# Nineteen column groups of an input projection by Strassen's seven products, ahead of the attention, their results kept in DRAM

## Chip, cores, metric

The kernel runs on one core of a Trainium2 chip. The metric is device time in microseconds (us): the median of the runs of one launch. Engines: PE (TensorE), DVE (VectorE), ACT (ScalarE), POOL (GpSimd), SP (SyncE, which here only issues DMAs).

## The reference

An encoder block on 1024 tokens of 1024 channels, all float32. A modulated RMSNorm gives `h`; one projection feeds two branches, which are merged by sigmoid gates, projected and added to the input.

```python
proj = h @ w_in        # 1024 x 9232
q_a, k_a, v_a, o_a, z_a, gates, q_b, k_b, v_b, z_b, g_merge = split(proj)
q_a, k_a = split(silu(conv3(concat(q_a, k_a))))
h_a = sigmoid(o_a) * bidirectional_mlstm(q_a, k_a, v_a, gates)   # 4 heads of 256
y_a = rms_norm_per_head(h_a) * silu(z_a)
y_b = neighbourhood_attention(q_b, k_b, v_b) * silu(z_b)         # 8 heads of 64
gm = sigmoid(g_merge + b_merge)                                  # two branches
merged = gm[0] * (y_a @ w_proj_a) + gm[1] * (y_b @ w_proj_b)
out = rms_norm(x + gate * (merged @ w_out))
```

The mLSTM is computed by chunks of 256 tokens: within a chunk as masked scores, between chunks through a state C of 256 x 256 a head, forward and backward.

## The kernel before

Every matrix product is made from float32 operands split in a high and a low part (`hi`, `lo`), as three PE products (`mm3`); `h` is held transposed as eight tiles `hhi`, `hlo` [128 channels, 1024 tokens]. `w_in` comes in groups of 256 columns. SP loads two of the eight row tiles at a time (`wraw`), ACT makes `whi`, POOL makes `wlo`. `dense_cm` computes a group channel-major, with moving operands of 512 columns (96 matmuls, four PSUM banks `dps`), `dense_tm` token-major, with moving operands of 256 columns (192 matmuls).

The PE order is written by the program (`manual_schedule`); the other engines' orders are made by a scheduler, and each engine works its instructions off in that order. The PE order comes from `weave`: it emits a **fill**, the dense groups, and between their steps the parts of the **chains** (generators), each when the lag it asked for, counted in us of emitted matrix work, has passed, or when a named flag is set. Where the fill waits for a flag, the chain's parts follow each other with nothing in between.

The stages, by PE's order:

- `front`: the norm, `h` and the gate columns, with the first group (`QB`, `KB` of pair 0).
- `na`: the attention. Chain `na_chain`: 64 blocks of 128 queries, each `na_scores` (tile `sps`, one bank; DVE adds the bias and takes the maximum, ACT the exponential, DVE normalises into `pt`), `na_weights` (three transposes `tps`, ACT and DVE split them into `ptr`) and `na_values` (`ops`). Fill `na_fill`: for each of four pairs a `VB`/`ZB` group, a merge gate group `gmerge(1, pair)`, the next pair's `QB`/`KB` group, at last `gmerge(0, 0)`.
- `projb`: branch B's projection, ahead of it `gmerge(0, 1)`; the chain `gates` makes the mLSTM's decays.
- `branch_a`: the mLSTM. Chain `mlstm`, for each head: backward states (`kps` transposes, `kweighted`, `state_step` into `cps`), then chunks c = 0 to 3 (`ml_scores` into `sps`, `Dm` and its split `pm`; products with the states and with v into `ips`; numerators `num`, divisors `rd`, sum `hout`). Fill `ml_fill`: per head K, V, Q groups, of the head before the O and Z groups (`gated_out`, token-major, whose evacuations apply the gates and the norm), and two `gmerge(0, ..)`.
- `proj_a`, `out_proj`: projection, merge, output projection, final norm.

The lags that set how closely chain parts stand:

```python
LAG = 1.1
NLAG = 0.6
```

Of the kernel before, what the change touches and what calls it, by code (L numbers as in the profile page):

```python
# [12 lines left out]
F32 = mybir.dt.float32  # L13
# [6 lines left out]
P = 128  # L20
# [25 lines left out]
class Build:  # L46
# [4 lines left out]
    # ---------------------------------------------------------------- helpers  # L51
# [96 lines left out]
    def dense_cm(self, src, cols, rhs, evac, nk=NK, nst=NST):  # L148
        """As dense_cm_steps, each bank in turn over a part's nst rows of tiles."""
# [16 lines left out]

    def dense_tm(self, src, cols, lhs, evac):
        """Token-major: 256 columns; bank b holds token tiles 2b and 2b+1."""
# [20 lines left out]
    # ---------------------------------------------------------------- constants  # L189
# [48 lines left out]
    # ---------------------------------------------------------------- adaLN RMSNorm, h^T  # L238
    def front(self, cols):
        """h^T, with the first projection (256 columns) and that of the gates following its tiles."""  # L240
        nc, io = self.nc, self.io
        got = []
        with self.pool("fr", bufs=2) as fp:
            wv = io["w_ada"].rearrange("(p j) (s k n) -> p j s k n", j=8, s=3, k=8)
# [90 lines left out]
            def h_high(s):  # L335
                x, m = xnT[:, 0, s], md[0]
                self.v0 = fp.tile([P, 512], F32, name="v0")
# [14 lines left out]
            xnT = fp.tile([P, NK, T], F32, name="xnT", bufs=1)  # L352
# [111 lines left out]
            self.constants()  # L464
# [20 lines left out]
    def gate_rows(self, ps):  # L485
        """Pre-activations, a row per direction and head; the backward ones in reversed time.
        Those of the lo parts of the weights lie four rows on."""
        nc = self.nc
        self.li = self.ybp.tile([40, T], F32, name="li")
        self.lz = self.ybp.tile([40, T], F32, name="lz")  # L490
# [80 lines left out]
    def out_gate(self, fp):  # L571
        """Half the residual gate as a row in DRAM."""
# [32 lines left out]
    # ---------------------------------------------------------------- neighbourhood attention  # L605
    def na(self, first, gps, ps0, ps1, fill):
        nc, io = self.nc, self.io
        self.yb = [self.ybp.tile([P, T], F32, name=f"yb{p}") for p in range(4)]
        with self.pool("na") as np_:
# [7 lines left out]
            for a in range(2):  # L617
                for h in range(2):
                    self.na_qk(0, a, h, first[a])
            self.gate_rows(gps)  # L620
            ps0.close()
# [5 lines left out]
    def na_fill(self):  # L627
        io = self.io
        for pair in range(4):
# [4 lines left out]
            yield from self.gmerge(1, pair)  # L634
            if pair < 3:
                yield from self.dense_cm(io["w_in"], [(QB + (pair + 1) * P, P), (KB + (pair + 1) * P, P)], self.hT,
                                         lambda a, h, banks: self.na_qk(pair + 1, a, h, banks))
# [46 lines left out]
    def na_chain(self):  # L684
        """Blocks of 8 columns of queries of each head: scores, then weights, then values."""
# [49 lines left out]
    def na_head(self, pair, hh):  # L735
        """Tables of 8 * bias + mask, rows of keys beside those of queries."""
# [94 lines left out]
    def projb(self, pp):  # L831
# [6 lines left out]
        yield from self.gmerge(0, 1)  # L838
# [15 lines left out]
    # ---------------------------------------------------------------- mLSTM  # L854
    def conv(self, mp, banks, ct, out):
        """3-tap convolution over tokens and x * (1 + tanh(x / 2)), which is 2 silu(x)."""
        nc = self.nc
        up = mp.tile([P, T + 2], F32, name="up", tag="up", bufs=2)
        nc.gpsimd.memset(up[:, 0:1], 0.0)
        nc.gpsimd.memset(up[:, T + 1:T + 2], 0.0)  # L860
        for h in range(2):
            nc.scalar.copy(up[:, 1 + h * 512:513 + h * 512], banks[h])
        yc = mp.tile([P, T], F32, name="yc", tag="yc")
# [472 lines left out]
```

## Time and profile before

| | |
|---|---|
| runs | 1330.67, 1331.93, 1332.37 us (median 1331.93) |
| profiled execution, first to last instruction | 1329.1 us |
| PE busy | 1305.2 us, 98%, 7560 matmuls |
| DVE, ACT, POOL busy | 651.8, 566.7, 418.5 us |
| HBM traffic | 92.48 MB read, 20.08 MB written |

The profiled execution gives its span; the median of the runs is 2.8 us above it. The costliest groups are the matmuls into `dps` (the dense groups). A matmul's duration in the profile holds its way through the array, so the pace of a row of matmuls is read from start to start.

### The profile page before, as it was taken

What the parts mean: (1) busy time and instruction counts of PE and PEld (TensorE: products, weight loads), DVE (VectorE), ACT (ScalarE), POOL (GpSimd) and SP (SyncE); (2) the same over time, 40 slices, a digit from 0 to 9 for tenths busy, and PEclk for the clock granted to TensorE, in tenths of its full rate; (3) what the DMA queues carried; (4) which work ended last, traced back from release to release, by engine and by line L of the source; (5) the groups of instructions that cost most, each with busy time, mean ns of one, the idle gap of its engine ahead of it and who ended that gap; (6) DMA issues with size and microseconds to landing.
All of it is one profiled execution on the core that took longest, in us unless ns stands there. A gap on an engine that the chain in (4) does not pass through costs nothing.

```text
span 1329.1 us, 19861 instructions
## 1 busy us (share of the span) xinstructions
PE 1305.2 (98%) x7560; PEld 1127.5 (85%) x7560; DVE 651.8 (49%) x1381; ACT 566.7 (43%) x1191; POOL 418.5 (31%) x381
## 2 busy tenths in 40 slices
PE   8799999999999899999999999999999999999997
PEld 8677777777777688988999989999989989888886
DVE  6944536435345441347626654555625641533533
ACT  6564434334444412336424553364434543423322
POOL 2634434335324423222212222222222212153332
PEclk9999999999999999999999999999999999999999
DMA  9633222222223364112111121112111122446432
GB/s 291 155 88 92 72 61 72 76 56 72 69 66 95 107 208 119 48 41 72 46 42 44 45 73 48 41 44 77 40 40 45 44 80 86 160 136 196 160 101 89
DMA packets 106187, 116.24 MB, mean 87 GB/s; under 512 B 9724, under 2 KB 86012, under 8 KB 106092
## 3 DMA queue, kind: packets, MB, share of 16 engines
q1 hardware_dynamic: 97352, 102.69, 27.1%
q10 hardware_dynamic: 8740, 12.29, 2.7%
q8 instruction: 59, 0.97, 0.3%
q14 instruction: 36, 0.29, 0.1%
HBM read 92.48 MB, written 20.08 MB: 85 GB/s over the span
## 4 chain that ended last, share of the span: by engine, by line
PE 91%; DMA 3%; DVE 2%; SPq 1%; ACT 1%; issue 1%; POOL 0%; ACTq 0%; POOLq 0%; DVEq 0%
PE dps L79 67%; PE ops L79 8%; PE ips L79 5%; PE sps L79 4%; PE cps L79 3%; PE tps L83 1%; PE wps L83 1%; DMA t_d<-gtmp 1%; SPq L251 1%; DMA wor<-in_w_out 1%; DMA wa<-in_w_ada 1%; PE kps L83 0%; PE ytp L83 0%; DVE acc L280 0%; PE gaps L79 0%
## 5 line engine op out<-in xcount | busy, mean ns | idle before, releaser
L74 POOL TENSOR_TENSOR wlo<-wraw,whi 128x512 fp32r<-128x512 f32 x168 | 227.0, 1351 | 585.9 <-ACT whi L73 576.0
L79 PE MATMUL dps<-hhi,whi 128*128 128x512 f32 x768 | 318.7, 415 | 1.0 <-ACT gtmp L827 0.6
L79 PE MATMUL dps<-hhi,wlo 128*128 128x512 f32 x768 | 302.6, 394 | 0.0
L79 PE MATMUL dps<-hlo,whi 128*128 128x512 f32 x768 | 298.8, 392 | 0.0
L79 PE MATMUL dps<-whi,hhi 128*128 128x256 f32 x768 | 217.1, 283 | 0.0
L79 PE MATMUL dps<-wlo,hhi 128*128 128x256 f32 x768 | 217.1, 283 | 0.0
L79 PE MATMUL dps<-whi,hlo 128*128 128x256 f32 x768 | 217.0, 283 | 0.0
L73 ACT ACTIVATE whi<-wraw 128x512 fp32r<-128x512 f32 x168 | 105.6, 629 | 228.6 <-PE dps L79 186.5
L79 PEld LDWEIGHTS dps<-hhi,whi 128*128 128x128 f32 x768 | 145.3, 189 | 32.2 <-issue 10.6
L79 PEld LDWEIGHTS dps<-hhi,wlo 128*128 128x128 f32 x768 | 145.2, 189 | 32.3
L79 PEld LDWEIGHTS dps<-hlo,whi 128*128 128x128 f32 x768 | 145.3, 189 | 18.6 <-DVE hlo L342 0.4
L79 PEld LDWEIGHTS dps<-wlo,hhi 128*128 128x128 f32 x768 | 146.9, 191 | 0.2
L79 PEld LDWEIGHTS dps<-whi,hhi 128*128 128x128 f32 x768 | 146.9, 191 | 0.2
L79 PEld LDWEIGHTS dps<-whi,hlo 128*128 128x128 f32 x768 | 146.9, 191 | 0.0
L79 PE MATMUL dps<-ya,whi 128*128 128x512 f32 x256 | 79.3, 391 | 0.0
L768 ACT ACTIVATE pt<-pt,mx 128x384 f32<-128x384 f32 (+1 forms) x64 | 37.7, 589 | 94.6 <-DVE mx L766 94.2
L1052 POOL TENSOR_TENSOR dg<-negm,mmask 128x256 f32<-128x256 f32 x32 | 25.0, 781 | 98.7 <-issue 28.9
L79 PEld LDWEIGHTS dps<-ya,whi 128*128 128x128 f32 x256 | 47.6, 188 | 9.7 <-DVE t0r L1182 0.2
L79 PE MATMUL ops<-woh,mlo 128*128 128x512 f32 (+1 forms) x136 | 51.3, 377 | 0.0
L79 PE MATMUL ops<-wol,mhi 128*128 128x512 f32 (+1 forms) x136 | 51.2, 377 | 0.0
L79 PE MATMUL ops<-woh,mhi 128*128 128x512 f32 (+1 forms) x136 | 51.2, 377 | 0.0
L79 PE MATMUL dps<-ya,wlo 128*128 128x512 f32 x128 | 49.9, 389 | 0.0
(265 smaller groups left out, 2359.1 us busy)
## 6 DMA issues: line engine op xcount, KB each, us to landing
wraw<-in_w_in SPq DMA_DIRECT2D x112, 256.0 KB
wa<-in_w_ada SPq DMA_DIRECT2D x16, 512.0 KB
wraw<-in_w_in SPq DMA_DIRECT2D x64, 128.0 KB
t_d<-gtmp ACTq DMA_DIRECT2D x32, 256.0 KB
xt<-in_x SPq DMA_DIRECT2D x8, 512.0 KB
wag<-in_w_ada SPq DMA_DIRECT2D x16, 256.0 KB
t1r<-t_d SPq DMA_DIRECT2D x8, 512.0 KB
mp_d<-t1r SPq DMA_DIRECT2D x16, 256.0 KB
```

What stands on the lines that cost most here:

```text
L73: nc.scalar.activation(hi, raw, AF.Copy)
L74: nc.gpsimd.tensor_tensor(lo, raw, f32(hi), op=ALU.subtract)
L79: self.nc.tensor.matmul(out, lhsT=lhsT, rhs=rhs, start=start, stop=stop, skip_group_check=True)
L83: self.nc.tensor.transpose(out, src, ident)
L251: nc.sync.dma_start(wa[:, :, s, :], wv[:, :, s, k, :])
L768: nc.scalar.activation(p_, p_, AF.Exp, bias=mx, scale=-1.0, accum_out=sm)
L1052: nc.gpsimd.tensor_tensor(dg, negm.rearrange("p (a b) -> p a b", a=2), mk, op=ALU.add)
```

## The change

Nineteen groups (three of `gmerge(1, ..)`, and K, O, Q, Z of four heads) are computed right after the front, before the attention, by Strassen's scheme (Winograd's form). `h` is cut in four quarters (channels by tokens), a group of `w_in` likewise; `combos` makes four sums of quarters of `h` once, as hi and lo; `st_set` computes one group by seven products of 12 matmuls, each 512 columns wide. Each group's result goes through its `put` function (tanh, silu or the convolution) to DRAM: `t_d`, `o_d`, `z_d`, `k_d`, `q_d`. `gmerge(1, 0)` is the front's group now, `gmerge(0, 1)` follows the front, and pair 0's `QB`/`KB` group begins the attention's fill. In the mLSTM only V remains a dense group (`values`). K and Q come back by chunk (`chunk`), O and Z too, in a new `gated_out`, spawned as a chain of its own after each chunk: O is transposed on PE (`otp`), multiplied in, squared, normed, and transposed back (`ytp`).

```diff
@@ new, called before the attention
+    def combos(self, x):
+        for k in range(4):
+            a11, a12, a21, a22 = x(k, 0), x(k + 4, 0), x(k, 1), x(k + 4, 1)
+            t = [sp.tile([P, 512], F32, name="part", tag="part", bufs=6) for _ in range(4)]
+            nc.vector.tensor_tensor(t[0], a22, a21, op=ALU.subtract)
+            nc.vector.scalar_tensor_tensor(t[1], t[0], -1.0, a11, op0=ALU.mult, op1=ALU.subtract)
+            nc.vector.tensor_tensor(t[2], a11, a21, op=ALU.subtract)
+            nc.vector.scalar_tensor_tensor(t[3], t[1], -1.0, a12, op0=ALU.mult, op1=ALU.subtract)
+            for i in (1, 0, 2, 3):
+                hi, lo = [s[:, k] for s in self.S[i]]
+                nc.scalar.activation(hi, t[i], AF.Copy)
+                (nc.gpsimd if i % 2 else nc.vector).tensor_tensor(lo, t[i], f32(hi), op=ALU.subtract)
+    def st_set(self, c0, put, psum):
...
+        x = bank()
+        yield from product(x, split(w11), quarter(0, 0), True)
+        p1 = copied(x)
+        y = bank()
+        yield from product(y, split(w21), quarter(1, 0), True)
+        put(0, 0, y, p1, False)
+        t1 = total(w11, w12)
+        t2 = total(t1, w22)
+        yield from product(x, split(t2), summed(1), False)
...
+        put(0, 1, x, None, False)
+    def ahead(self):
...
+            for g in range(1, 4):
+                do(GM + 1024 + g * 256, self.put_tanh(self.t_d[1], g, 8 + g * 2))
+            for hd in range(HEADS):
+                do(KA + hd * 256, self.put_conv(self.k_d[hd], 8 + hd * 2))
+                do(OA + hd * 256, self.put_tanh(self.o_d, hd, None))
+                do(QA + hd * 256, self.put_conv(self.q_d[hd], hd * 2))
+                do(ZA + hd * 256, self.put_silu(hd))
@@ na_fill
+        yield from qk(0)
         for pair in range(4):
...
             if pair:
                 yield f"na{pair - 1}"
-            yield from self.gmerge(1, pair)
             if pair < 3:
...
@@ projb
-        yield from self.gmerge(0, 1)
@@ mlstm
-        nxt = self.ml_split(mp, 0, qT, kT)
+        nxt = self.ml_split(mp, 0, qd, kd)
...
+            self.spawn(self.gated_out(mp, hd, c, hout))
@@ gated_out, now by chunk
+        for src, n in ((self.o_d, "oc"), (self.z_d, "zc")):
+            t = mp.tile([P, 2, L], F32, name=n, bufs=2)
+            nc.sync.dma_start(t, src[hd * 256:(hd + 1) * 256, s].rearrange("(a p) t -> p a t", p=P))
...
+        yield 3.0
...
+                self.transpose(tp[:, i, dt], oz[0][:, dt, i * P:(i + 1) * P], self.ident)
+        for i in range(2):
+            nc.vector.scalar_tensor_tensor(hout[:, i], tp[:, i].rearrange("p a b -> p (a b)"), 1.0, hout[:, i], op0=ALU.add, op1=ALU.mult)
+            so = mp.tile([P, 256], F32, name="so", bufs=2)
+            nc.scalar.activation(so, hout[:, i], AF.Square, accum_out=ssq[:, i:i + 1])
+        self.rsqrt(rstd, ssq, 1.0 / HD, 4 * EPS, mp, 2)
+        for i in range(2):
+            nc.scalar.activation(hout[:, i], hout[:, i], AF.Copy, scale=rstd[:, i:i + 1])
+        last = hd == HEADS - 1
+        yield "ya" if last else 6.0
...
@@ ml_fill
-        gm = [[2], [], [], [3]]
-        for hd in range(HEADS):
-            yield from self.qkv(mp, hd)
-            if hd:
-                yield from self.gated_out(mp, hd - 1)
-            for g in gm[hd]:
-                yield from self.gmerge(0, g)
-        yield "ml3"
-        yield from self.gated_out(mp, 3)
+        yield from self.values(mp, 0)
+        yield from self.values(mp, 1)
+        yield from self.gmerge(0, 2)
+        for hd in range(2, HEADS):
+            yield f"ml{hd - 2}"
+            yield from self.values(mp, hd)
+            if hd == 3:
+                yield from self.gmerge(0, 3)
```

Three places of the built program. In the attention, PE's order of the kernel before, in the middle of pair 0 (`dps` are steps of the fill, the rest is the chain):

```order
L79 MATMUL dps<-hhi_104,whi 128x512
L79 MATMUL dps<-hlo_105,whi 128x512
L79 MATMUL dps<-hhi_104,wlo 128x512
L79 MATMUL sps<-kB,qA 128x384
L79 MATMUL sps<-kl,qA 128x384
L79 MATMUL dps<-hhi_90,whi 128x512
L79 MATMUL dps<-hlo_91,whi 128x512
L79 MATMUL dps<-hhi_90,wlo 128x512
L83 MATMUL tps<-ident,pt 128x128 x3
```

PE's order of the change, near the end of pair 0:

```order
L79 MATMUL ops<-ptr_3952,vb 128x256
L79 MATMUL ops<-ptr_3953,vb 128x256
L79 MATMUL sps<-kB,qA 128x384
L79 MATMUL sps<-kl,qA 128x384
L83 MATMUL tps<-ident,pt 128x128 x3
L79 MATMUL ops<-ptr_3952,vb 128x256
L79 MATMUL ops<-ptr_3953,vb 128x256
L79 MATMUL sps<-kB,qA 128x384
L79 MATMUL sps<-kl,qA 128x384
```

The fill stands no longer between the parts of some blocks: five at the end of each pair, and the last blocks' weights and values behind them.

In the mLSTM, PE's order of the kernel before in chunk 2 of head 0 (products with the backward state, then the state's update):

```order
L79 MATMUL ips<-sb2h,qsh 128x258
L79 MATMUL ips<-sb2l,qsh 128x258
L79 MATMUL ips<-sb2h,qsl 128x258
L79 MATMUL dps<-hhi_94,whi 128x512
L79 MATMUL dps<-hlo_95,whi 128x512
L79 MATMUL dps<-hhi_94,wlo 128x512
L79 MATMUL cps<-vhi,kwh 128x258
L79 MATMUL cps<-vlo,kwh 128x258
```

PE's order of the change at the same place:

```order
L79 MATMUL ips<-sb2h,qsh 128x258
L79 MATMUL ips<-sb2l,qsh 128x258
L79 MATMUL ips<-sb2h,qsl 128x258
L79 MATMUL ips<-sb2h,qsh 128x258
L79 MATMUL ips<-sb2l,qsh 128x258
L79 MATMUL ips<-sb2h,qsl 128x258
L79 MATMUL cps<-vhi,kwh 128x258
L79 MATMUL cps<-vlo,kwh 128x258
```

The steps of the fill between the two are gone; the next `dps` stands after the last chunk of the head.

ACT's order of the change in a chunk without fill (head 1, chunk 2; in brackets whose work each waits for):

```order
L1226 ACTIVATE so,hssq<-hout 128x256 [waits DVE_49] x2
L1229 ACTIVATE hout<-hout,hrstd 128x256 [waits Activation_49,Pool_49]
L1229 ACTIVATE hout<-hout,hrstd 128x256 [waits Activation_49]
L1163 ACTIVATE hout<-num,rd 128x256 [waits DVE_49]
L1137 ACTIVATE num<-ips,col_6842 128x258 [waits PE_49]
L1137 ACTIVATE num<-ips,col_6842 128x258 [waits PE_49,Activation_49]
L1056 ACTIVATE qsh<-qc 128x512
```

The two scalings by `hrstd`, which come from the new `gated_out` of the chunk before and wait for POOL's root, stand ahead of this chunk's `num` and of `qsh`, which the next chunk's scores need.

## Rows read from the trace of the kernel before

**Rows 1.** The page: span, and part 1's row of PE.
```profile
span 1329.1 us, 19861 instructions
...
PE 1305.2 (98%) x7560; PEld 1127.5 (85%) x7560; DVE 651.8 (49%) x1381; ACT 566.7 (43%) x1191; POOL 418.5 (31%) x381
```
**Rows 2.** The chain of waits in order of time: start us, us, what, count.
```profile
148.80 16.34 PE dps L79 x72
...
611.01 1.42 PE sps L79 x12
...
626.58 1.43 PE sps L79 x12
...
1098.74 42.86 PE dps L79 x358
```
**Rows 3.** PE in order of time (start us, us), four transposes and what follows.
```profile
724.27 0.60 PE L83 MATMUL kps<-ident,kT 128*128 128x128 f32 x4
...
724.62 0.36 PE L79 MATMUL dps<-whi,hhi 128*128 128x256 f32 x1
```
**Rows 4.** Busy time by stretches, two chunks of head 0.
```profile
611.00:627.00 16.00, 16.00 (x105) 14.53 (x104) 12.96 (x35) 9.21 (x22) 4.32 (x4) 1.00 0.26 67
627.00:643.00 16.00, 16.00 (x105) 14.54 (x104) 9.84 (x30) 8.21 (x19) 2.71 (x3) 1.00 0.14 33
```
**Rows 5.** DVE and POOL in order of time, chunk 1 of head 0.
```profile
611.96 1.52 DVE L1026 SCALAR_TENSOR_TENSOR hout<-num,rd,hout 128x256 f32<-128x256 f32 x1
613.40 0.41 DVE L1059 SCALAR_TENSOR_TENSOR Dm<-sps,Dm 128x256 f32<-128x256 f32 x1
...
614.61 0.56 DVE L915 TENSOR_TENSOR pml<-Dm,pmh 128x384 fp32r<-128x384 f32 x1
615.08 0.68 DVE L915 TENSOR_TENSOR ksl<-kT,ksh 128x512 fp32r<-128x512 f32 x1
...
627.38 0.48 DVE L1026 SCALAR_TENSOR_TENSOR hout<-num,rd,hout 128x256 f32<-128x256 f32 x1 [0.45 <-ACT hout L1024]
...
611.90 1.30 POOL L74 TENSOR_TENSOR wlo<-wraw,whi 128x512 fp32r<-128x512 f32 x1 [6.69 <-ACT whi L73]
```
**Rows 6.** Groups by line and shape, the whole span: count, busy us, mean ns.
```profile
L1078 DVE SCALAR_TENSOR_TENSOR hout<-so,hout 128x256 f32<-128x256 f32 x32 | 12.1, 420 | 24.6 <-ACT so L1077 24.6
...
L998 ACT ACTIVATE num<-ips,col 128x258 f32<-128x258 f32 x48 | 22.5, 469 | 16.0 <-PE ips L79 11.6 <-ACT yt L1115 2.6 <-issue 1.1
...
L1024 ACT ACTIVATE hout<-num,rd 128x256 f32<-128x256 f32 x32 | 16.3, 509 | 35.8 <-DVE rd L1022 35.6
...
L1079 ACT ACTIVATE so<-hout 128x256 f32<-128x256 f32 x32 | 13.1, 413 | 1.3 <-DVE hout L1078 1.3
...
L236 POOL TENSOR_TENSOR rstd<-rsq,mhalf 128x1 f32<-128x1 f32 x8 | 5.1, 678 | 15.0 <-DVE rsq L235 14.2 <-DVE md L304 0.8
```
**Rows 7.** DVE in order of time, one block of the attention.
```profile
201.06 0.56 DVE L766 CUSTOM_DVE_ANT_0 pt<-sps,tint 128x384 f32<-128x384 f32 x1 [1.01 <-PE sps L79]
...
202.66 0.42 DVE L771 TENSOR_SCALAR pt<-pt,rc 128x384 f32<-128x384 f32 x1
203.00 0.55 DVE L785 TENSOR_TENSOR ptr<-tps,ptr 128x384 fp32r<-128x384 f32 x1
204.57 0.56 DVE L766 CUSTOM_DVE_ANT_0 pt<-sps,tint 128x384 f32<-128x384 f32 x1 [1.02 <-PE sps L79]
```
**Rows 8.** Groups of POOL by line and shape, end of the attention and branch B's split.
```profile
L814 POOL TENSOR_TENSOR yb<-osum,zz 64x512 f32<-64x512 f32 x16 | 20.6, 1290 | 36.0 <-DVE osum L813 26.0 <-PE tps L83 5.5 <-PE dps L79 4.4
...
L837 POOL TENSOR_TENSOR yblo<-yb,ybhi 128x1024 fp32r<-128x1024 f32 x4 | 9.5, 2390 | 0.0
```
**Rows 9.** The page's part 5: the splits of the weights.
```profile
L74 POOL TENSOR_TENSOR wlo<-wraw,whi 128x512 fp32r<-128x512 f32 x168 | 227.0, 1351 | 585.9 <-ACT whi L73 576.0
...
L73 ACT ACTIVATE whi<-wraw 128x512 fp32r<-128x512 f32 x168 | 105.6, 629 | 228.6 <-PE dps L79 186.5
```
**Rows 10.** Busy time by stretches in the front; after the five engines the granted clock.
```profile
30.00:33.00 3.00, 3.00 (x11) 2.32 (x9) 2.82 (x10) 1.22 (x2) 0.06 (x1) 0.50 0.88 220
...
39.00:57.00 18.00, 13.35 (x64) 10.30 (x63) 17.76 (x33) 9.28 (x15) 11.42 (x8) 1.00 0.64 156
```

More of the change, by code (lines that the diff above doesn't have):

```diff
@@ new lines, in st_set, with total, split, quarter @@
+    def st_set(self, c0, put, psum):
+        nc, sp, S = self.nc, self.sp, self.S
+        raw = [self.sw.tile([P, 4, 256], F32, name="raw", tag="raw", bufs=4) for _ in range(2)]
+        for i, r in enumerate(raw):
+            nc.sync.dma_start(r, self.io["w_in"][i * 512:(i + 1) * 512, c0:c0 + 256].rearrange("(k p) c -> p k c", p=P))
+        (w11, w12), (w21, w22) = [[r[:, :, n * P:(n + 1) * P] for n in range(2)] for r in raw]
+        def total(a, b):
+            t = self.sw.tile([P, 4, P], F32, name="wsum", tag="wsum", bufs=3)
+            nc.vector.tensor_tensor(t, a, b, op=ALU.add)
+            return t
+        def split(src):
+            hi = self.wp.tile([P, 4, P], F32R, name="whi", tag="whi", bufs=WSPL)
+            lo = self.wp.tile([P, 4, P], F32R, name="wlo", tag="wlo", bufs=WSPL)
+            nc.scalar.activation(hi, src, AF.Copy)
+            nc.gpsimd.tensor_tensor(lo, src, f32(hi), op=ALU.subtract)
+            return hi, lo
+        def quarter(kh, h):
+            return lambda k: [t[k + 4 * kh][:, h * 512:h * 512 + 512] for t in (self.hhi, self.hlo)]
+        def summed(i):
+            return lambda k: [t[:, k] for t in S[i]]
+        def product(bank, w, a, start):
+            for k in range(4):
+                self.mm3(bank, [t[:, k] for t in w], a(k), start and k == 0, k == 3)
+                yield 0
+        def copied(bank):
+            t = sp.tile([P, 512], F32, name="part", tag="part", bufs=6)
+            nc.scalar.copy(t, bank)
+            return t
+        def bank():
+            return psum.tile([P, 512], F32, name="dps", tag="d")
+        x = bank()
[7 more added lines that the diff above has]
+        yield from product(x, split(t2), summed(1), False)
+        u2 = copied(x)
+        z = bank()
+        yield from product(z, split(t1), summed(0), True)
+        p5 = copied(z)
+        yield from product(x, split(total(w12, w22)), summed(2), False)
+        put(1, 1, x, p5, True)
+        yield from product(z, split(w22), summed(3), False)
+        put(1, 0, z, u2, True)
+        yield from product(x, split(total(t2, w21)), quarter(1, 1), False)
+        put(0, 1, x, None, False)
@@ new lines, in joined, with do @@
+    def joined(self, out, bank, part, neg):
+        nc = self.nc
+        if neg:
+            nc.vector.scalar_tensor_tensor(out, bank, -1.0, part, op0=ALU.mult, op1=ALU.subtract)
+        else:
+            nc.vector.tensor_tensor(out, bank, part, op=ALU.add)
+    def ahead(self):
+        n = 0
+        with self.pool("psx", bufs=4, space=PSUM) as psx:
+            def do(c0, put):
+                nonlocal n
+                n += 1
+                for _ in self.st_set(c0, put, (self.psd, psx)[n % 2]):
+                    pass
+            for g in range(1, 4):
[5 more added lines that the diff above has]
+                do(ZA + hd * 256, self.put_silu(hd))
@@ new lines, in put_conv, with put @@
+    def put_conv(self, dst, ct):
+        nc, st = self.nc, {}
+        def put(m, h, bank, part, neg):
+            if m not in st:
+                st[m] = self.sw.tile([P, T + 2], F32, name="up", tag="up", bufs=2)
+                nc.gpsimd.memset(st[m][:, 0:1], 0.0)
+                nc.gpsimd.memset(st[m][:, T + 1:T + 2], 0.0)
+                half = st[m][:, 1 + h * 512:513 + h * 512]
+                self.joined(half, bank, part, neg)
+                return
+            half = st[m][:, 1 + h * 512:513 + h * 512]
+            if part is None:
+                nc.scalar.copy(half, bank)
+            else:
+                self.joined(half, bank, part, neg)
+            self.conv(st[m], ct + m, dst[:, m])
+        return put
@@ L603, in out_gate, with na @@
             yield 1.5
-    def na(self, first, gps, ps0, ps1, fill):
+    def na(self, ps1, fill):
         nc, io = self.nc, self.io
@@ L628, in na_fill, with qk @@
         io = self.io
+        def qk(pair):
+            return self.dense_cm(io["w_in"], [(QB + pair * P, P), (KB + pair * P, P)], self.hT,
+                                 lambda a, h, banks: self.na_qk(pair, a, h, banks))
+        yield from qk(0)
         for pair in range(4):
@@ L633, in na_fill @@
                 yield f"na{pair - 1}"
-            yield from self.gmerge(1, pair)
             if pair < 3:
-                yield from self.dense_cm(io["w_in"], [(QB + (pair + 1) * P, P), (KB + (pair + 1) * P, P)], self.hT,
-                                         lambda a, h, banks: self.na_qk(pair + 1, a, h, banks))
+                yield from qk(pair + 1)
                 yield f"S{pair}"
@@ L942, in ml_chain @@
         for hd in range(HEADS):
[L943 removed]
+            yield from self.mlstm(mp, hd, LAG)
             self.flags.add(f"ml{hd}")
```

230 lines of the change are left out of this document (119 added, 111 removed).

## Prediction

> **What bounds the kernel now.** I read the page first: PE is busy 98% of a span of 1329.1 us [rows 1], so the matrix work alone sets the time, as long as there is other matrix work whenever a chain waits. The chain of waits says at which pace: 72 matmuls of 512 columns take 16.34 us, 0.227 each; 358 of 256 columns take 42.86 us, 0.120 each [rows 2]. Half the columns cost a little more than half. The busy times by stretches then show what the other engines do under this cover: in a chunk of the mLSTM some 16 us long PE has no gap, while DVE is busy 12.96 and 9.84 us, ACT 9.21 and 8.21 [rows 4]. From scores to scores that chunk takes 626.58 - 611.01 = 15.6 us [rows 2]. PE's own order has 66 chain matmuls in it (7.9 us at 0.12); the other 7.7 us are 33 matmuls of fill. That fill is what the change takes away.
>
> **The change, part by part.**
>
> *Matrix work.* PE's order has 2304 dense matmuls of 256 columns before and 768 after; of 512 columns 2304 before (h with w_in) and 2844 after. So 1536 x 0.120 = 183.9 us go and 540 x 0.227 = 122.5 come. (12 of each 96 are Strassen's saving; O and Z besides go from token-major to channel-major.) New are 64 transposes of O: four take 0.35 us from the first's start to the next matmul [rows 3], 16 x 0.35 = 5.6. Net 55.8 us less: 1329.1 - 55.8 = **1273.3** if PE stayed as full.
>
> *Start.* Behind the front, `gmerge(0, 1)`'s third part of weights is split by ACT only after 4 tanh, 8 gate rows and 8 high parts of the sums, 20 instructions of about 0.65 us (128 x 512 takes 0.63, [rows 9]), 13 us, then itself (0.6) and POOL (1.35); PE is there after 48 x 0.227 = 10.9. That is a wait of 4 us, and 3 more for the later parts: **+7** (0 to 15). The sums themselves (24 DVE instructions near 0.7) end about when the first summed product is due, 27 us behind the front.
>
> *The Strassen stage.* A set is 84 x 0.227 = 19.1 us of PE. POOL splits seven weights, 7 x 1.35 = 9.5; ACT has about 9, DVE up to 14 in a K or Q set and 5 in the others. All are covered, so I charge only jitter at bank reuse, a quarter of a us a set: **+5** (0 to 15).
>
> *Attention.* `gmerge(1, ..)` is no longer fill here; five blocks at the end of each pair stand bare, 20 in all. In a block DVE starts on the scores at 201.06 and has normalised them at 203.08, 2.0 us, of which PE must wait for the transposes [rows 7]. The block before takes 204.57 - 201.06 = 3.5 us for itself and three fill steps of 3 x 3 x 0.227 = 2.05, so PE's own part of a block is at most 1.45; I take 1.35. With one bank for scores, the next block's scores and then this block's transposes follow each other, so that two blocks hold one such path and twice PE's part: period (2.0 + 1.35) / 2 = 1.7, a little more by DVE's order, say 1.85; 20 x 0.5 = 10. The last blocks' values drain bare, 3 more: **+13**. Bounds of the term: 5, if DVE's four instructions of a block, some 1.6 us from start to start, set the pace (20 x 0.25), and 25, at 2.5 us a block, that is half of the path on top of PE's part.
>
> *Branch B.* `gmerge(0, 1)` covered the split of `yb`. Now, after the last value product, come its sum, POOL's product (1.29), then four `yblo` of 2.39 one after the other [rows 8]; PE can start at the first but not finish k = 1 before the second. About 8 us idle, of which the kernel before already had some: **+6** (0 to 15).
>
> *mLSTM.* This is the large term. The order after the change has four runs of chain matmuls without any `dps` between: 156, 228, 186 and 177 matmuls, with 116 transposes (29 groups): 747 x 0.12 + 29 x 0.35 = 100 us of PE. They hold chunks 1 to 3 of head 0, all of head 1, 1 to 3 of head 2 and the backward states of head 3, and 1 to 3 of head 3. How long does a bare chunk take? Bounded below by PE, 7.9 + 0.7 = 8.6; by DVE, the mean of the two stretches, 11.4 [rows 4], less about 1 for the instruction that POOL held up (1.52 against 0.48, [rows 5]), plus the new gating, 2 x 0.42 and 2 x 0.47 and 0.15, so 12.3. Above by 15.6, the paced chunk, in which nothing waited. Between them I follow one path through the orders of the change, scores to next scores: scores 1.42 [rows 2]; DVE's four Dm products and divisions between 1.8, `hout` 0.5, two `pml` 0.95, `yt` 0.9, `kwl` 0.45, `ksl` 0.6 (start to start, [rows 5]), C 0.45, the products with O 0.85, 6.5 together; ACT's second square 0.6; root 0.15 on DVE and 0.7 on POOL; ACT's two scalings 0.85, `hout` 0.5, two `num` 0.95, `qsh` 0.63 [rows 6, 9]; `qsl` 0.7; ten hand-overs at 0.1. That is **14.0**. The new root sits on this path, since ACT takes its instructions in order and the scalings stand ahead of `num` and `qsh`. Whole chunks 14, first ones 13, last ones 11 (no state, no next split), three backward steps 10: 35 + 52 + 45 + 39 = 171 us, against 100: **+71** (at DVE's 12.3: +50; at the paced 15.6: +92).
>
> The row behind the 12.3: DVE's `hout`, 1.52 us long at 611.96, ran beside POOL's `wlo` from 611.90 to 613.20; the same shape took 0.48 at 627.38 [rows 5]. In bare stretches POOL splits no weights. The Trainium skill (SBUF — State Buffer, "Who interferes with whom") states that a DVE instruction with two SBUF inputs contends with a GpSimd one that reads SBUF, and the second to issue blocks wholly. That agrees with the row; by it DVE's short durations hold in the bare chunks. Were the mean durations of the whole trace used instead, the path would be 1 us longer and this term about 12 us larger.
>
> *End.* After head 3's last chunk: numerators and `hout`, gate product, squares, root, scaling, transposes, split, only then `proj_a`'s last part; about 9 us against 2 before: **+7** (3 to 12).
>
> Sum: 1273.3 + 7 + 5 + 13 + 6 + 71 + 7 = 1382.3 us of span. The median of the runs lies 2.8 above the profiled span, so **1385 us**, 4% slower.
>
> **The rivals.**
>
> A. *The chains overlap themselves.* If DVE and ACT worked on one chunk while PE is in the next, bare chunks would cost PE's 8.6 us and blocks PE's 1.35: no +71, no +10. Then 1385 - 81 = 1304, faster. It decides from where the bare chunk falls under about 10 us (with the attention as summed, break-even is 53 us less than the forecast, 171 - 53 = 118 us for the four runs). For it: PE's order gives each chunk four banks and the engines were 30% idle. Against: DVE's own 12.3 us a chunk, which no order shortens, and one buffer for `qs`. 7%.
>
> B. *The clock falls in the bare runs.* In the front the granted clock was 0.50 in a stretch of transposes and few matmuls (11 in 3 us), but 1.00 over 18 us in which PE was busy 13.35 [rows 10]; a bare chunk has PE busy 8.6 of 14. At half clock the 100 us of PE become 200, of which I take half as hidden by DVE: +50, 1435. The Trainium skill (TensorE: Matmul & The Clock Gate, "Why this matters for your kernels") warns against idle gaps between bursts of matmuls; here the gaps are single microseconds. 10%.
>
> C. *Strassen's stage is bound elsewhere.* If a K or Q set is held by DVE (14 us of work, each contended by POOL's 9.5) the eight of them could take 24 us instead of 19: +40, 1425. For it: the contention of rows 5. Against: O and Z sets between, and banks to run ahead. 8%.
>
> That the change doesn't do what it says is excluded by the counts of matmuls in the order.
>
> **How the numbers follow.** The forecast (bare chains wait on DVE and ACT, 12.3 to 15.6 a chunk) has 75%: 1364 to 1406 by that term alone, 1345 to 1420 with the others' bounds. The rest is 7% for A, 10% for B, 8% for C. The range 1342 to 1428 takes in the forecast's own range and C, and leaves out A and most of B. Faster by over 0.2% (about what a measurement can tell from no change): 0.08, A and a little of the forecast's lower tail; within 0.2%: 0.02; slower: 0.90.
>
> **What would show it.** PE's busy share near full until the last blocks of each attention pair, then in the mLSTM four stretches of 35 to 52 us with PE some 60% busy, ended by V groups or by `proj_a`. In them, waits of PE for `qsl`, `kwl` and DVE's sums of `num`; DVE busy near 90%; ACT waiting for POOL's `hrstd`. Scores to scores 13 to 15 us. Granted clock 1.00 there (B: 0.50). In the Strassen stage 84 matmuls in 19 to 19.5 us (C: more in K and Q sets). The prediction is wrong if scores follow each other in 10 us or less, or if the time is lost before the mLSTM begins.

## The result, and the profile after

The changed kernel takes **1431.48 us** (median; 1430.47 to 1432.14), the kernel before beside it 1332.15: ratio 1.0746, interval 1.0731 to 1.0761. It is slower, as forecast, but by 99 us where the forecast was 53, and 3.5 us above the range. The profiled execution has a span of 1429.8 us. The page, its first part's row of PE and the granted clock of its second (compare [rows 1]):

```profile
span 1429.8 us, 18853 instructions
...
PE 1311.3 (92%) x6628; PEld 1088.9 (76%) x6628; DVE 785.1 (55%) x1550; ACT 625.7 (44%) x1289; POOL 522.3 (37%) x458
...
PEclk9999999999999999898979979999999999789999
```

PE's 98% have become 92%, and the clock dips five times where it stood at 9 throughout before: at the end of each of the four attention pairs, and in the mLSTM's last head. Busy times by stage tell where (start, Strassen stage, attention from its first scores, branch B, mLSTM; columns as in [rows 4]: length, then PE, PE's loads, DVE, ACT, POOL with counts, clock, DMA share, GB/s):

```profile
39.90:113.40 73.50, 59.29 (x241) 46.01 (x242) 54.00 (x73) 40.81 (x66) 42.56 (x34) 0.93 0.40 114
113.40:491.40 378.00, 362.95 (x1561) 294.82 (x1560) 210.41 (x207) 152.60 (x252) 187.72 (x160) 0.99 0.29 97
529.00:834.10 305.10, 276.44 (x1213) 208.11 (x1211) 160.18 (x409) 128.96 (x301) 114.07 (x89) 0.90 0.21 57
834.10:914.40 80.30, 77.28 (x446) 66.44 (x447) 36.08 (x48) 25.97 (x44) 29.88 (x23) 0.94 0.59 182
914.40:1262.10 347.70, 303.05 (x2061) 279.03 (x2059) 217.14 (x621) 198.91 (x480) 65.62 (x72) 0.95 0.36 107
```

PE's busy time still hides much, since a matmul's duration stretches while it waits and at the lower clock. So I take the matmuls of each stage at their own pace (0.227 us for 512 columns, 0.173 for 384, 0.12 for 256, 0.088 for a transpose) and call the rest of the stage's length **lost**:

| term of the sum | forecast | lost after less lost before | |
|---|---|---|---|
| matrix work | -55.8 | -56.1 | 540 x 0.227 - 1536 x 0.12 + 64 x 0.088, by the matmuls in both traces |
| start | +7 | +13.6 | 42.9 - 29.3 |
| Strassen stage | +5 | +24.1 | from its first sum to its last |
| attention | +13 | +40.0 | 73.7 - 33.7 |
| branch B | +6 | +7.4 | 17.0 - 9.6 |
| mLSTM and tail | +71 + 7 | +72.5 | 79.1 - 6.6 |
| sum | +53.2 | +101.5 | spans: 1429.8 - 1329.1 = 100.7; the paces are rounded |

The largest term was right. The 47 us that the forecast lacks lie in the attention (27), in the Strassen stage (19) and at the start (7); the mLSTM and its tail took 6 less than forecast.

**The attention.** PE in order of time, the end of pair 0 (idle time before, and who ended it, in brackets):

```profile
575.12 0.34 PE L79 MATMUL sps<-kB,qA 128*128 128x384 f32 x1
...
576.75 0.34 PE L79 MATMUL sps<-kB,qA 128*128 128x384 f32 x1
...
579.93 0.52 PE L83 MATMUL tps<-ident,pt 128*128 128x128 f32 x3 [2.48 <-DVE rc L938]
...
580.67 0.52 PE L79 MATMUL sps<-kB,qA 128*128 128x384 f32 x1
...
583.08 0.52 PE L79 MATMUL sps<-kB,qA 128*128 128x384 f32 x1
...
585.50 0.88 PE L83 MATMUL tps<-ident,pt 128*128 128x128 f32 x3 [1.28 <-DVE pt L939]
...
586.92 0.52 PE L79 MATMUL sps<-kB,qA 128*128 128x256 f32 x1
...
591.11 0.79 PE L79 MATMUL dps<-hhi,whi 128*128 128x512 f32 x1 [3.16 <-DVE kl L827]
591.70 0.63 PE L79 MATMUL dps<-hlo,whi 128*128 128x512 f32 x1
592.13 0.63 PE L79 MATMUL dps<-hhi,wlo 128*128 128x512 f32 x1
```

From 576.75 to 583.08 two blocks take 6.3 us and the next one 3.8, where the forecast had 1.85 a block. From the first of these scores (575.12) to the fifth (586.92) it is 11.8 us for four blocks; the other pairs took 10.7, 11.8 and 11.0 there, so 2.8 a block on average. Every second block's transposes wait, for DVE. What DVE and ACT did for the block of 580.67, in order of time, and then ACT's part in a covered block of the kernel before [rows 7]:

```profile
581.85 0.56 DVE L934 CUSTOM_DVE_ANT_0 pt<-sps,tint 128x384 f32<-128x384 f32 x1 [0.28 <-PE sps L79]
...
582.68 0.49 ACT L952 ACTIVATE ptr<-tps 128x384 fp32r<-128x384 f32 x1 [1.70 <-PE tps L83]
...
583.07 0.60 ACT L936 ACTIVATE pt<-pt,mx 128x384 f32<-128x384 f32 x1
...
584.25 0.56 DVE L934 CUSTOM_DVE_ANT_0 pt<-sps,tint 128x384 f32<-128x384 f32 x1 [0.50 <-PE sps L79]
...
584.93 0.42 DVE L939 TENSOR_SCALAR pt<-pt,rc 128x384 f32<-128x384 f32 x1
```

```profile
201.72 0.61 ACT L768 ACTIVATE pt<-pt,mx 128x384 f32<-128x384 f32 x1 [2.41 <-DVE mx L766]
...
202.34 0.47 ACT L784 ACTIVATE ptr<-tps 128x384 fp32r<-128x384 f32 x1
```

From its scores (581.85) to its normalised weights (585.35) this block takes 3.5 us on the two engines, where the covered block took 2.0: in the covered block ACT makes the exponential first and then the split of the block before, here the split stands first; and DVE turns to the next block's scores (584.25), which PE has not yet finished, before it normalises.

At the pair's end comes a wait that it did not have at all: the next fill group needs the four banks that the next pair's Q and K hold, and these can leave only after the last scores (586.92) have let go of the one buffer of Q and K. After it matmuls stand 0.43 apart (591.70 to 592.13) instead of 0.227: that is the pace of the lower clock, 1.2 GHz (granted 0.50). In the attention PE waits 15.5 us in front of transposes (7.3, 6.5 and 1.7 us in the list of its waits) and 9.5 for the banks; the other 15 of the 40 us are in no wait of that list. By the granted clock, 0.90 over 305 us, some 60 us of the stage ran at the lower level (an estimate).

**The Strassen stage.** All engines in order of time, around one of eight stalls:

```profile
436.60 2.32 DVE L329 SCALAR_TENSOR_TENSOR yc<-up,conv_w_sb,yc 128x1024 f32<-128x1024 f32 x1
...
437.86 2.20 POOL L204 TENSOR_TENSOR wlo<-raw,whi 128x512 fp32r<-128x512 f32 x1
...
440.53 1.27 DVE L330 SCALAR_TENSOR_TENSOR yc<-up,conv_w_sb,yc 128x1024 f32<-128x1024 f32 x1
...
441.70 0.39 PE L79 MATMUL dps<-s0hi,wlo 128*128 128x512 f32 x1
...
441.90 1.06 ACT L331 ACTIVATE up<-yc 128x1024 f32<-128x1024 f32 x1 [4.13 <-DVE yc L330]
...
442.86 0.61 ACT L281 ACTIVATE part<-part 128x512 f32<-128x512 f32 x1
...
443.38 0.57 ACT L220 COPY part<-dps 128x512 f32<-128x512 f32 x1
...
444.00 0.78 PE L79 MATMUL dps<-s2hi,whi 128*128 128x512 f32 x1 [1.91 <-ACT part L220]
...
444.58 0.63 PE L79 MATMUL dps<-s2lo,whi 128*128 128x512 f32 x1
```

PE waits for a copy out of the bank that it wants to accumulate into. The copy stands in ACT's order behind the tanh of a convolution, and that tanh waits 4.13 us for DVE, whose product of 1024 elements takes 2.32 us beside POOL's split and 1.27 alone. The list of PE's waits in this stage has a single row:

```profile
PE dps L79 <- ACT part L220: 15.0, 8, 1.9
```

**The mLSTM.** The four runs without fill, and PE's longest waits in the second (us in total, times, longest):

```profile
970.30:1002.00 31.70, 26.09 (x178) 24.08 (x178) 24.68 (x79) 21.61 (x61) 6.70 (x8) 0.89 0.45 130
1031.80:1073.90 42.10, 35.37 (x256) 32.57 (x255) 35.63 (x120) 31.24 (x83) 8.72 (x10) 0.96 0.37 103
1137.00:1181.60 44.60, 33.74 (x228) 29.61 (x227) 34.50 (x112) 33.06 (x88) 8.67 (x11) 0.96 0.56 160
1206.40:1262.10 55.70, 36.39 (x212) 33.18 (x210) 33.02 (x112) 29.23 (x76) 6.23 (x8) 0.80 0.16 48
```

```profile
PE sps L79 <- ACT qsh L1056: 2.4, 2, 1.4
PE sps L79 <- DVE qsl L1057: 1.7, 3, 1.1
PE cps L79 <- DVE kwl L1067: 1.5, 1, 1.5
```

Together 174.1 us; the forecast was 171. A whole bare chunk, scores to scores, lasts 1064.48 - 1051.66 = 12.8 us in head 1:

```profile
1051.66 0.38 PE L79 MATMUL sps<-qsh,ksh 128*128 128x256 f32 x1 [1.01 <-ACT qsh L1056]
...
1064.48 0.39 PE L79 MATMUL sps<-qsh,ksh 128*128 128x256 f32 x1 [1.41 <-ACT qsh L1056]
```

The waits of PE are those named, for `qsh`, `qsl` and `kwl`. Between these scores ACT waits for POOL's root, ahead of `hout`, `num` and `qsh` in its order:

```profile
1061.88 0.91 ACT L1229 ACTIVATE hout<-hout,hrstd 128x256 f32<-128x256 f32 x2 [1.20 <-POOL hrstd L404]
...
1063.81 0.62 ACT L1056 ACTIVATE qsh<-qc 128x512 fp32r<-128x512 f32 x1
```

So the path by way of ACT's order stands in front of the next scores, as forecast.

### The profile page after: what moved, and what is told of

It reads as the page before. It is cut to its first block, busy times and chain, and to the rows that moved or that the text cites. A ratio compares the mean times of both kernels' runs of the same rounds, so it can differ in the third digit from the quotient of the medians.

```text
span 1429.8 us, 18853 instructions
## 1 busy us (share of the span) xinstructions
PE 1311.3 (92%) x6628; PEld 1088.9 (76%) x6628; DVE 785.1 (55%) x1550; ACT 625.7 (44%) x1289; POOL 522.3 (37%) x458
## 3 DMA queue, kind: packets, MB, share of 16 engines
q1 hardware_dynamic: 117416, 122.61, 29.3%
## 5 line engine op out<-in xcount | busy, mean ns | idle before, releaser
L79 PE MATMUL dps<-hhi,whi 128*128 128x512 f32 x644 | 266.1, 413 | 14.9 <-DVE kl L827 9.5
L79 PE MATMUL dps<-hhi,wlo 128*128 128x512 f32 x644 | 255.1, 396 | 0.9 <-POOL wlo L204 0.9
L74 POOL TENSOR_TENSOR wlo<-wraw,whi 128x512 fp32r<-128x512 f32 x92 | 122.3, 1331 | 289.0 <-ACT whi L73 278.1
L204 POOL TENSOR_TENSOR wlo<-wsum,whi 128x512 fp32r<-128x512 f32 x76 | 106.6, 1404 | 110.4 <-ACT whi L203 110.4
L73 ACT ACTIVATE whi<-wraw 128x512 fp32r<-128x512 f32 x92 | 57.6, 627 | 116.8 <-PE dps L79 83.9
L204 POOL TENSOR_TENSOR wlo<-raw,whi 128x512 fp32r<-128x512 f32 x57 | 82.9, 1458 | 53.1 <-ACT whi L203 53.1
L203 ACT ACTIVATE whi<-wsum 128x512 fp32r<-128x512 f32 x76 | 47.6, 630 | 84.9 <-PE dps L79 82.1
L79 PE MATMUL dps<-whi,hhi 128*128 128x256 f32 x256 | 73.5, 287 | 0.0
L79 PE MATMUL dps<-whi,hlo 128*128 128x256 f32 x256 | 72.4, 283 | 0.0
L79 PE MATMUL dps<-wlo,hhi 128*128 128x256 f32 x256 | 72.4, 283 | 0.0
```

Source lines behind the costliest of these rows:

```text
L73: nc.scalar.activation(hi, raw, AF.Copy)
L74: nc.gpsimd.tensor_tensor(lo, raw, f32(hi), op=ALU.subtract)
L79: self.nc.tensor.matmul(out, lhsT=lhsT, rhs=rhs, start=start, stop=stop, skip_group_check=True)
L203: nc.scalar.activation(hi, src, AF.Copy)
L204: nc.gpsimd.tensor_tensor(lo, src, f32(hi), op=ALU.subtract)
```

## The experiments

The times are medians; the change is 1431.5.

**Attention: thinner fill** (`na_thin`). The order said that some fill is spent early, three steps a block, and the last five blocks get none.

```diff
@@ na_chain
                 self.na_weights(heads[(i - 1) // 8], (i - 1) % 8)
-                yield NLAG
+                yield 0.0
```

> In the attention two steps of fill a block instead of three (no lag between weights and values); by PE's order no block stands bare any more, the matrix work is the same. Theory 1 (the attention's extra loss of 40 us is the 20 bare blocks, with the wait for the evacuations of Q and K behind them and the halved clock): 25 to 40 us less than 1431. Rival (blocks 2.7 us apart are too close for DVE and ACT, so that PE waits in every block): less than 10 us gained, or slower.

1419.0 us, 12 less. No block stands bare, but only a third of the 40 us comes back. PE now goes from the last scores straight into the wait for the banks, which has grown:

```profile
582.09 0.38 PE L79 MATMUL sps<-kl,qA 64*128 64x256 f32 x1
586.63 0.79 PE L79 MATMUL dps<-hhi,whi 128*128 128x512 f32 x1 [4.16 <-DVE qA L824]
```

**Two buffers for Q and K as well** (`na_qk2`).

```diff
@@ na_qk (kB, kl alike), osum, na_fill
-            qA = np_.tile([P, 2, T], F32R, name="qA")
+            qA = np_.tile([P, 2, T], F32R, name="qA", bufs=2)
...
-            t = self.np_.tile([P, 4, P], F32, name="osum", tag="osum", bufs=3)
+            t = self.np_.tile([P, 4, P], F32, name="osum", tag="osum", bufs=2)
...
-                yield f"S{pair}"
```

> As the thinner fill of the attention (two steps a block), and Q, K and K's low part of a pair get two buffers, so that the next pair's Q and K can leave PSUM before this pair's last scores; the fill no longer waits for these scores (the sums of the value products keep two buffers instead of three). Theory 2 (of the attention's 40 us, the thinner fill took away the bare blocks, 12 to 14 us; what is left is the wait at each pair's end, 4.2 us, for the four banks that Q and K hold, and the slow matmuls behind it): 12 to 20 us less than that run's 1419, so 1400 to 1407. Rival (the next pair's Z group meets the same wait for this pair's last values): within 4 us of 1419.

1408.7 us, 10 less again (12 to 20 expected): the waits for `kl` and `qA` at the pairs' ends are gone. What the attention has lost more than in the kernel before has gone from 40 to 14 us.

**The merge gate groups back** (`gm_back`), with one buffer and the old lags.

```diff
@@ ahead
-            for g in range(1, 4):
-                do(GM + 1024 + g * 256, self.put_tanh(self.t_d[1], g, 8 + g * 2))
@@ na_fill
             if pair < 3:
+                yield from self.gmerge(1, pair + 1)
                 yield from qk(pair + 1)
```

> The change, but the three merge gate groups of the attention are dense groups of its fill again instead of Strassen sets ahead of it (8.2 us more matrix work); by PE's order only the last pair's five blocks stand bare. Theory 1 (the attention's extra loss of 40 us is the lost cover: the blocks, about 3.4 us each where PE needs 1.35, and the wait for the banks of Q and K at each pair's end): three of four pairs win 8 to 10 us, so 1431 - 27 + 8 = 1412, between 1405 and 1418. Rival (the loss lies in blocks and waits that cover does not touch): 1435 to 1442.

1408.5 us, within what was expected, although this kernel has 8 us more of matrix work: in the attention 32 of the 40 us come back.

**Matmuls that nobody needs** (`na_busy`) in five blocks a pair, to keep PE and its clock up.

```diff
@@ na_weights
-        tp = self.psm.tile([P, 3, P], F32, name="tps", tag="pt", bufs=1)
+        tp = self.psm.tile([P, 4, P], F32, name="tps", tag="pt", bufs=1)
         n = len(kbs)
+        if hd["hh"] == 1 and b > 2:
+            for _ in range(12):
+                self.nc.tensor.matmul(tp[:, 3], lhsT=self.hhi[0][:, 0:P], rhs=self.hhi[0][:, 0:P], start=True, stop=True, skip_group_check=True)
```

> Twelve matmuls of 128 columns more in each of the last five blocks of each pair, into columns that nobody reads, at the place where PE waits for the normalised weights. They add matrix work and nothing else. Theory 1 (in the bare blocks half of the loss is the granted clock, 0.50 there, which falls because PE idles): the clock stays at 1.00 until the last block, 8 to 20 us less than 1431 in spite of the added work. Rival (the blocks wait for DVE and ACT, PE's clock makes no difference): within 4 us of 1431. Rival (the added matmuls delay the transposes): up to 20 us slower.

1458.2 us, 27 more. The clock did what theory 1 says (1.00 up to the wait for the banks), the time did not. The same stretch of pair 0, first the change, then this kernel:

```profile
582.00:585.00 3.00, 2.22 (x7) 1.38 (x6) 1.68 (x7) 1.17 (x4) 0.56 (x1) 0.50 0.00 0
585.00:588.00 3.00, 2.45 (x9) 1.96 (x9) 1.51 (x5) 1.64 (x5) 0.00 (x0) 0.50 0.00 0
```

```profile
582.00:585.00 3.00, 2.72 (x20) 2.21 (x20) 1.59 (x5) 1.20 (x3) 0.54 (x1) 1.00 0.00 0
585.00:588.00 3.00, 2.41 (x20) 2.08 (x19) 1.54 (x8) 2.07 (x5) 0.00 (x0) 1.00 0.00 0
```

At either clock it is 14 us from the scores near 576.7 to the end of the wait for the banks (591.11 and 590.66). This does not show that the clock costs nothing in the blocks, for the run changed more than the clock. Only the first of its transposes there still waits for DVE; the next two start 2.4 and 2.6 us after their weights are normalised, behind the twelve added matmuls (1.56 us). And in its second block DVE's path is 2.0 us again, with the exponential ahead of the split in ACT's order. What the full clock would win without the added matmuls stays open. The 27 us are the added matmuls where they stand beside fill, in the slow stretch behind the stall (12 of them took 2.65 us there), and in the last pair, whose blocks went from 3 to 5 us.

**Strassen stage: copies on DVE** (`copy_dve`).

```diff
@@ st_set, copied
-            nc.scalar.copy(t, bank)
+            nc.vector.tensor_copy(t, bank)
```

> The copies of three of the seven products out of PSUM go to DVE instead of ACT. Theory 1 (in each of the sets after a K or Q set PE waits 1.9 us for such a copy, which stands in ACT's order behind a tanh that waits for DVE's convolution; with the slow matmuls after it 2.9 us): eight waits gone, 15 to 23 us less than 1431. Rival (the convolution on DVE, slowed by POOL's splits, holds the copies as long in DVE's own order): within 5 us of 1431.

1452.8 us, 21 more: the rival, and further than it said. PE's waits in the stage:

```profile
PE dps L79 <- DVE part L220: 29.2, 12, 3.2
```

DVE's order holds the copies longer than ACT's did, so ACT is not the engine that is late.

**No silu** (`no_silu`).

```diff
@@ conv
-        nc.scalar.activation(up[:, 0:T], yc, AF.Tanh, scale=0.5)
-        nc.vector.scalar_tensor_tensor(yc, up[:, 0:T], 1.0, yc, op0=ALU.add, op1=ALU.mult)
```

> K and Q go to DRAM without the silu behind the convolution: ACT's tanh and DVE's product with it are left out, 16 of each, so that K and Q aren't the reference's. Theory 1 (PE's stalls in the Strassen stage are ACT's order, in which the tanh that waits for DVE stands ahead of the copy): the stage takes 15 to 24 us less, 1407 to 1416. Rival (DVE's three products alone hold the sums of the weights and the joins): less than 8 us gained.

1410.9 us, 21 less, as theory 1 has it; the stage loses 3.4 us instead of 24. With no tanh in ACT's order that waits for DVE, the copies are in time, though DVE's three products are still there. DVE also has one of its four instructions less, of 1.2 us, so this run alone does not tell the tanh's place from DVE's load.

**One product on ACT** (`tap_act`).

```diff
@@ conv
-        nc.vector.tensor_scalar(yc, up[:, 1:T + 1], w[:, 1:2], self.convb[:, ct:ct + 1], op0=ALU.mult, op1=ALU.add)
+        nc.scalar.activation(yc, up[:, 1:T + 1], AF.Identity, scale=w[:, 1:2], bias=self.convb[:, ct:ct + 1])
```

> The first of the convolution's three products goes from DVE to ACT. Theory 3 (the stalls of 1.9 us come from DVE, whose products beside POOL's splits take 2.2 us instead of 1.3, so that ACT's tanh waits and the copies behind it; 2.4 us less of DVE ahead of the second tanh): 8 to 23 us less than 1431. Rival (ACT's order is the limit, and one instruction of 1 us more makes it later): 0 to 15 us slower.

1419.2 us, 12 less; the stage loses 9.1 us:

```profile
PE dps L79 <- ACT part L220: 6.2, 6, 1.5
```

Less DVE ahead of the tanh, less wait. The reading that fits all three runs: DVE is late with the products, and the copy stands behind them, in ACT's order by way of the tanh, in `copy_dve` directly.

**mLSTM: the fill spread** (`ml_lag`).

```diff
-LAG = 1.1
+LAG = 0.3
```

> LAG 0.3 instead of 1.1 in the mLSTM: one step of fill between two chain parts instead of two or four, so that the same V groups and merge gate groups last longer. By PE's order the four runs without fill (863 matmuls and transposes) become two (133 and 182). Theory 1 (what the mLSTM lost, 72 us over the kernel before, is bare chain time, about 12.8 us a chunk, and the amount of fill suffices if it is spread): 25 to 45 us less than the change's 1431. Rival (the chains are so slow that they set the end wherever the fill stands): within 10 us of 1431. Rival (backward states and first chunks, which now have less cover, lose as much as the later ones win): within 10 us, with new waits of PE in the backward states.

1424.3 us, 7 less: the rivals. The bare runs are shorter, but PE waits elsewhere: 1.2 to 2.3 us for `kwh` in the backward states, which had more fill before, and 3.55 for `pmh` in head 2's last chunk. The last head's transposes still wait 12.9 us. To lay the same fill thinner gave back a tenth of what the stage had lost.

**Backward states beside the chunks** (`ml_two_lag`), on top of it.

```diff
@@ ml_chain, mlstm
+    def ml_back(self, mp):
+        for hd in range(HEADS):
+            yield f"v_{hd}"
+            yield 2.0
+            yield from self.back(mp, hd, LAG)
+            self.flags.add(f"b_{hd}")
...
-                kw = self.kweighted(mp, kt[:, c - 1] if c else ps, c, rowf)
+                kw = self.kweighted(mp, self.kps(kc), c, rowf)
@@ branch_a
             self.spawn(self.ml_chain(mp))
+            self.spawn(self.ml_back(mp))
```

> In the mLSTM the backward states become a chain of their own, which runs beside the chunks of the head before (own buffers for its weighted K and its states; K is transposed again for each chunk instead of kept; LAG 0.3 as in that run). Theory 1 (the mLSTM lasts as long as its chains, about 82 us a head, of which the backward states are 25 to 30; PE and DVE have room): three heads' backward states lie beside the chunks before, 30 to 55 us less than that run's 1424. Rival (DVE or ACT is the limit, or the four PSUM banks, which both chains now share): less than 12 us gained.

1417.3 us, 7 less than that run, less than the rival's bound. In the mLSTM and its tail some 63 us are lost instead of 71, and the 32 added transposes bring 2.8 us of matrix work. Theory 1 fails by its size: two chains side by side win 8 us, not 30. To make room the run also took buffers away (`hout` from four to three, the chunks of Q from three to two). Whether these, the four banks or another engine hold the rest was not separated.

**The last head's transposes** (`ytp_late`).

```diff
@@ gated_out
-        yield "ya" if last else 6.0
+        if last:
+            yield "ya"
+        yield 6.0
```

> The change with one edit: the last head's gated chunks get the lag of 6.0 ahead of their second transposes, as the other heads have it, once the projection has begun. Theory (PE, which works in order, waits 5.6, 4.5 and 3.0 us at these transposes for the chunk's root and scaling, while the next chunk's products stand behind them): 6 to 12 us less than 1431. Rival (the head is held by its chain, so the wait only moves): within 4 us.

1421.4 us, 10 less: in the last head the flag is set already and so left no lag. In the change PE waited so at four such rows, 17.6 us in all; the longest:

```profile
1216.77 1.11 PE L83 MATMUL ytp<-ident,hout 128*128 128x128 f32 x4 [5.55 <-ACT hout L1229]
```

**Together, and fill given back** (`v1`): `na_qk2`, `tap_act`, the lag (3.0), LAG 0.6, and

```diff
@@ ahead, ml_fill
-                do(ZA + hd * 256, self.put_silu(hd))
+                if hd == 0:
+                    do(ZA + hd * 256, self.put_silu(hd))
...
-        yield from self.gmerge(0, 2)
...
+            yield from self.zgroup(mp, hd)
@@ projb
+            if g == 0:
+                yield from self.gmerge(0, 2)
```

> All findings together: thinner fill and two buffers for Q and K in the attention, the first product of the convolution on ACT, the last head's second transposes with a lag of 3; and fill given back to the mLSTM: three of the Z groups are dense groups there again (8.2 us more matrix work than by Strassen), the merge gate group of head 0 covers the start of branch B's projection, LAG 0.6, with which by PE's order no chunk stands bare. Theory (the loss is where chains stand bare; PE's order decides): 1431 less 23 (attention), 12 (Strassen stage), 55 to 65 (mLSTM and tail, from 72), 5 (branch B), plus 8: 1330 to 1350. Rival (DVE and ACT, which have more work than in the kernel before, hold the mLSTM with fill too): 1360 to 1380.

1366.9 us, 65 less than the change, ratio to the kernel before 1.0262 (1.0248 to 1.0276). It lies in the rival's range, 17 us above the theory's. The mLSTM and its tail lose 40 us instead of 79, and no chunk stands bare by PE's order. Of these 39 us some 13 are what the last head's lag won alone (that stage's loss in `ytp_late`), so cover gave back about a third of the 79 (an estimate from the two runs), and half of the loss stays with cover everywhere. The list of PE's waits has 12 us there, for `kwh`, `num` and `qsh` above all, in chunks that have fill between their parts; where the rest lies stays open.

**Other buffers at the start** (`v1_start`).

```diff
@@ run
-                        for _ in self.gmerge(0, 1):
+                        put = self.put_tanh(self.t_d[0], 1, 2)
+                        for _ in self.dense_cm(self.io["w_in"], [(GM + 256, 256)], self.hT, lambda m, h, banks: put(m, h, banks[h], None, False)):
```

> The same, and the merge gate group behind the front puts its results into the six buffers of the Strassen stage instead of two of its own. Theory (the start's 13 us are 5.3 of waiting for the first set's weights and the wait for the second, which both stand in ACT's order behind tanh instructions that wait for a buffer until its DMA has landed, 3.65 us): 4 to 8 us less than the run beside it. Rival (the weights wait for the sums of the quarters on DVE): within 2 us.

1365.9 us, 1.0 less, with ranges that overlap: the rival. The wait for the first set's weights is still there, 5.89 us. Their split stands in ACT's order behind the last high part of the sums, which DVE delivers late, and behind two tanh; whether the load of the weights would have been earlier was not tried. Ratio to the kernel before 1.0252 (1.0238 to 1.0266): the fastest of these kernels, and slower than the one that was there.

## Why the prediction was right and wrong

*Matrix work: right.* -56.1 against -55.8; the trace has exactly the matmuls that the order had.

*mLSTM: right in size and path, the size in part by luck.* 174 us for the four runs against 171. The parts balance: whole chunks took 11.1 to 13.8 instead of 14, but the last head's 17, because of the transposes without a lag, which stood in the order that I had. The end came out inside this term. What was expected of busy engines was wrong: DVE 127.8 of 174.1 us, 73% and not near 90, so the path through all engines is the bound and not DVE. The size as a sum over bare runs held, but `v1` has no bare chunk and still loses 40 us there, so "bare" is not the whole cause; the rest stays open.

*Attention: the step that failed is "two blocks hold one such path and twice PE's part: period (2.0 + 1.35) / 2".* That one wait comes in two blocks was right: the transposes at 579.93 and 585.50 wait, those at 581.74 do not. But the formula has PE's part once where the sentence has it twice, (2.0 + 2.7) / 2 = 2.35. And the 2.0 us were read in a covered block. In the bare blocks whose transposes wait, two in each pair, the path took 3.1 to 3.8 us, since other blocks' instructions stand in it in ACT's and DVE's orders (the rows above). With 3.5 the sentence gives 3.1 a block; the trace has 2.8, and 20 x (2.8 - 1.35) = 29 instead of 10. The one score bank, from which the forecast argued, was no wait of PE's: 0.2 us for scores in the whole stage. That the orders make the path long is read from the trace; no run changed them alone.

The second omission: the sum took the matrix work that leaves and the blocks that lose their cover, but not what that work stood in front of. Between this pair's last scores and the next group there had been a merge gate group; without it PE meets the banks of Q and K, 3.16 us at each of three pairs (9.5 of the 40). `na_qk2` takes this wait away, and `gm_back`, which puts the cover back, returns 32 of the 40 us. The upper bound of 25 (by its own 2.5 us a block it would be 23) had no room for either.

*Strassen stage: the step "all are covered, so I charge only jitter" failed.* The forecast compared each engine's load with PE's 19.1 us a set; the loads did fit. What does not fit is an order: a copy with the 2.7 us of one product's twelve matmuls as slack, behind a tanh that comes late. The eight stalls are 15.0 of the 24 us, and the slow matmuls after three of them some 5 more (an estimate from their spacing, 0.43 instead of 0.227); the other 4 are small gaps, about the jitter that was charged. Rival C had the place and the contention, but as load (24 us a set), which did not come: PE waits in the set after K or Q, not in it.

*Start: mis-sized*, 13.6 against 7, near the upper bound of 15: PE waits 5.3 us for the first set's weights, and in the front 9.9 for `acc` on DVE where it had waited 6.6. *Branch B: right*, 7.4 against 6.

*The rivals.* A fell with 12.8 us a chunk. B was half right: the clock fell, most of all where it was not looked for, in the attention (0.90 over the stage, 0.50 in the blocks), and to 0.80 in the last head. In the mLSTM, at 0.95 over 348 us, some 35 us ran at the lower level, which at twice the pace is at most 17 us of the 72.5 (an estimate); what of it PE's waits would have covered anyway was not separated, and `na_busy` does not settle it for the attention. The Trainium skill (TensorE: Matmul & The Clock Gate, "Why this matters for your kernels") warns against idle gaps between bursts of matmuls; the trace agrees that the clock falls behind stalls: it was at 0.50 from 582 on, behind the wait of 2.48 us that ended at 579.93.

## What to carry to other kernels

Work that covers others' waits is worth more than its own length: before it is made cheaper or moved, list what stands in front of it and behind it in PE's order, the banks that the next group needs among it. A path's length that is read where the path is covered need not be its length where it stands bare: go through each engine's order for what stands in it. An engine with room to spare can still be late: look in its order for what stands ahead of the one instruction that PE waits for.

## What the runs showed of the hardware

DVE's instructions with two operands in SBUF have mostly two durations here: of the 76 sums of weights of the Strassen stage 59 took 0.7 us and 16 took 1.7 to 1.8. Sums of 128 x 512 at the start of the change, in order of time:

```profile
93.31 0.68 DVE L179 TENSOR_TENSOR part<-xnT 128x512 f32<-128x512 f32 x1
...
94.12 1.62 POOL L184 TENSOR_TENSOR s1lo<-part,s1hi 128x512 fp32r<-128x512 f32 x1 [1.30 <-ACT s1hi L183]
...
94.51 1.78 DVE L184 TENSOR_TENSOR s0lo<-part,s0hi 128x512 fp32r<-128x512 f32 x1
...
95.69 1.75 POOL L184 TENSOR_TENSOR s3lo<-part,s3hi 128x512 fp32r<-128x512 f32 x1
```

0.68 us with POOL idle, 1.78 beside it, and POOL's 1.3 become 1.6 to 1.75. The Trainium skill (SBUF — State Buffer, "Who interferes with whom") states that the two contend for a shared pair of ports; the trace agrees. The forecast's sum had priced the first case alone.

The same stall of 1.9 us was followed by the lower clock three times in eight (in the rows above, durations of 0.78 and then 0.63 us behind 444.00, where 441.70 has 0.39), and five times not. And with twelve small matmuls in a block the clock stayed at 1.00 where it was 0.50 without them (the rows of that run above).
